# A hybrid decoder block on one core: the recurrence's coefficient on ScalarE, the input weights' low parts in two pieces on GpSimd

## The chip, the core and the metric

The kernel runs on one core of a Trainium2 chip. A core has five engines with queues of their own: TensorE (PE in the profile; its weight loads are PEld), VectorE (DVE), ScalarE (ACT), GpSimd (POOL) and SyncE (SP), which issues most of the DMAs. The metric is the device time of one execution in microseconds (us), as a median over runs.

## What is computed

The reference is one decoder block in float32 over 512 positions of 1024 channels. Cut to what matters here:

```
h = rmsnorm(x);  z = h @ w_in + b_in          # 1024 -> 6656 columns
z_glu, z_rx, z_rg, z_ga, z_gb = split(z)      # 2048, 1280, 1280, 1024, 1024
u  = glu(z_glu); u = causal depthwise conv, 31 taps; layernorm; silu
xb = causal depthwise conv of z_rx, 4 taps
r  = sigmoid(block_diag(wa) xb + ba);  i = sigmoid(block_diag(wx) xb + bx)
log_a = -8 * r * softplus(-lambda);  a = exp(log_a)
h_t = a_t * h_(t-1) + sqrt(1 - a_t^2) * (i * xb)_t          # the recurrence
y_a = u @ conv_w_out + b;  y_b = (h * gelu(z_rg)) @ lru_w_out
x  = x + (sigmoid(z_ga) * y_a + sigmoid(z_gb) * y_b) @ w_mix_out
x  = x + (silu(h2 @ w1) * (h2 @ w3)) @ w2;  out = rmsnorm(x)    # h2 = rmsnorm(x)
```

## The kernel before

Channels lie on the 128 partitions, the 512 positions along the free dimension. Every float32 operand of a product is split in two parts, a high one (a rounded copy in the format that TensorE multiplies) and a low one (the operand minus its high part). A product is then three matmuls: high by high, high by low, low by high.

The input product is done in 52 groups of 128 columns of z. A group is 8 slices of the contraction by 3 matmuls, 24 matmuls of 512 positions, into one PSUM bank (`mm3`, lines 534 to 546). There are six such banks in one pool, and two in another for the long convolution. The weights of a group come as one chunk of 128x1024 by a DMA that SP issues (line 175). `emit_chunk` asks ScalarE to copy the high part (line 124) and GpSimd to subtract for the low part (`split_to`, then `sub` on line 120). The weights are asked for four chunks ahead of their use (`AHEAD`), and there are four tiles of raw weights (`RAW`) and five of split ones (`HL`). The first two chunks, in the opening that is ordered by hand, are subtracted by GpSimd in halves already (`InHalves`, line 155). Chunks of later stages name VectorE for the low part.

The list `ORDER` interleaves the groups by kind: u (the gated input of the long convolution), rx (input of the short convolution and of the recurrence), g (the recurrence's gates), r (the recurrence itself), rg, gb and ga (the other branches). `beside` is a generator of the long convolution's steps: 31 taps by 8 tiles of channels on VectorE (line 743), of which a few are issued after each group. `make_out_sums` lets GpSimd add and subtract quarters of the last weight matrix in 256-column pieces (lines 447 and 120, tile `ows`), tied behind the newest subtraction of a chunk by `newest["sub"]`.

The function that the first half of the change touches is `gates(j)`, called ten times. Four to six matmuls per gate fill two banks, `r_` and `i_`, whose tile name in the profile is `g`. ScalarE takes tanh of both (lines 873, 874; a sigmoid as half of one plus tanh), then an exponential into the tile `A` (`ea` in the profile, line 877) and another tanh into the bank `r_` (line 878). VectorE forms (A + 1) * r_ in the bank (line 879), which is a - 1, and (i_ + 1) * xb (line 880). Line 881 writes the recurrence's coefficient a = r_ + 1 into `A`, and line 882 writes (A + 1) * r_ = a^2 - 1 into `th`. `recur(j)`, some groups later, takes the square root on ScalarE into a bank (line 890), multiplies by xb (line 891) and scans along the positions (line 892).

Only a few stretches are ordered by hand (`manual_schedule`: the opening and the ends of the mix product). Elsewhere the framework's scheduler writes each engine's queue beforehand, from the order of the program and from times that it estimates, and sets the semaphores for data, buffers and banks. On the chip each queue is executed in order. The rest of the block (the output products, the mix product in seven quarter products, the channel mixer likewise) follows in the same manner on the same engines.

Of the kernel before, what the change touches and what calls it, by code (L numbers as in the profile page):

```python
# [8 lines left out]
F32 = mybir.dt.float32  # L9
F32R = mybir.dt.float32r  # L10
AF = mybir.ActivationFunctionType
ALU = mybir.AluOpType

P = 128
T = 512
# [72 lines left out]
def tile_block(ctx, tc, a, out):  # L88
# [19 lines left out]
    def bank(name):  # L108
        return psum.tile([P, T], F32, tag="mm", name=name)
# [4 lines left out]
    vec, act, pe, pool_e = nc.vector, nc.scalar, nc.tensor, nc.gpsimd  # L114
# [4 lines left out]
    def sub(eng, o, x, y):  # L119
        return eng.tensor_tensor(out=o, in0=x, in1=y, op=ALU.subtract)  # L120

    def split_to(h, l, full, eng, copy=act.copy):

        copy(h, full)  # L124
        if eng is vec and "tie" in newest:
            with tc.issue_after(newest["tie"]):
                last = sub(eng, l, full, h.bitcast(F32))
        else:
            last = sub(eng, l, full, h.bitcast(F32))
        if eng is pool_e:  # L130
            newest["sub"] = last.ins
        return h, l, last

    def split(name, full, eng, p_=None, copy=act.copy):
        p_ = p_ or pairt(name)
        return split_to(*p_, full, eng, copy)[:2]
# [21 lines left out]
    def emit_chunk(copy=act.copy, lo_by=None):  # L158
        if emitted[0] == GATES_AT:
            load_gates()  # L160
        key, src, kt, cols, where, lo, after = chunks[emitted[0]]
        emitted[0] += 1
        lo = lo_by or lo
        n = kt * cols
        if where == "made":
            raw = src()
        else:
            raw = raws.tile([P, 1024], F32, tag="raw", name=f"raw_{key}")
        rv = raw[:, :n]
        if where == "made":  # L170
            pass
        elif callable(src):
            src(raw)
        else:
            newest["load"] = nc.sync.dma_start(rv.rearrange("p (k n) -> p k n", k=kt), src).ins
        if where != "long":
            hl = hls.tile([P, 2, 1024], F32R, tag="hl", name=f"hl_{key}")
            h, l, _ = split_to(hl[:, 0, :n], hl[:, 1, :n], rv, lo, copy)
            if after:
                after(rv, h)  # L180
            held[key] = (h.rearrange("p (k n) -> p k n", k=kt), l.rearrange("p (k n) -> p k n", k=kt))
        else:
            held[key] = [
                split_to(longt(f"{key}h{i}", F32R), longt(f"{key}l{i}", F32R), rv[:, i * T : (i + 1) * T], lo)
                for i in range(2)
            ]
# [5 lines left out]
    def weights(key, ahead=AHEAD):  # L192
        i = next(i for i, c in enumerate(chunks) if c[0] == key)
        emit_to(i + 1 + ahead)
        return held.pop(key)
# [657 lines left out]
    def gates(j):  # L853
        hv, lv = (gate_view(v[:, 0, :]) for v in weights(f"gate{j}"))
        j5 = j % 5
        banks = []
        for g in range(2):
            ps = bank(f"g{j}_{g}")
            (wh, oh), (wl, ol) = ((v[:, g, 0, :], v[:, g, 1, :]) for v in (hv, lv))
            xh, xl = xbp[j]  # L860
            mms = [(wh, xh), (wh, xl), (wl, xh)]
            if j5 % 2:
                eh, el = ext[j]
                mms += [(l[:MANY], r[:MANY]) for l, r in ((oh, eh), (oh, el), (ol, eh))]
            else:
                mms.append((oh[: 3 * FEW], ext[j][0][: 3 * FEW]))
            for k, (l, r) in enumerate(mms):
                pe.matmul(ps, l, r, start=k == 0, stop=k == len(mms) - 1)  # L868
            banks.append(ps)

        r_, i_ = banks
        th = gatet(f"th{j}")
        act.activation(th, r_, AF.Tanh, scale=0.5, bias=bh[:, 0, j : j + 1])
        act.activation(i_, i_, AF.Tanh, scale=0.5, bias=bh[:, 1, j : j + 1])

        A = gatet(f"ea{j}")
        act.activation(A, th, AF.Exp, scale=c8[:, j : j + 1], bias=c8[:, j : j + 1])
        act.activation(r_, th, AF.Tanh, scale=c4[:, j : j + 1], bias=c4[:, j : j + 1])
        vec.scalar_tensor_tensor(out=r_, in0=A, scalar=1.0, in1=r_, op0=ALU.add, op1=ALU.mult)
        vec.scalar_tensor_tensor(out=xb[j], in0=i_, scalar=1.0, in1=xb[j], op0=ALU.add, op1=ALU.mult)  # L880
        vec.tensor_scalar(out=A, in0=r_, scalar1=1.0, scalar2=None, op0=ALU.add)
        vec.scalar_tensor_tensor(out=th, in0=A, scalar=1.0, in1=r_, op0=ALU.add, op1=ALU.mult)
        rec[j] = A, th

# [25 lines left out]
    for kind, j in ORDER:  # L910
        next(sums_steps, None)
        if kind == "u":
            glu(j)
        elif kind == "rx":
            rx(j)
            run_beside(4)
        elif kind == "g":
            gates(j)
        elif kind == "r":
            recur(j)  # L920
        elif kind == "rg":
            rg(j)
            run_beside(6)
        elif kind == "gb":
            sig(GB, j, sgb, "sgb")
            run_beside(6)
        else:
            sig(GA, j, sga, "sga")
            run_beside(8)
# [237 lines left out]
    with tc.manual_schedule(engines={ET.PE}):  # L1167
        ws = w_tiles(f"f1_{PLAIN}", ND, 0)
        for q in range(4):
            cs, ks = HALVES[q // 2], range(4 * (q % 2), 4 * (q % 2) + 4)  # L1170
# [211 lines left out]
```

## Time and profile before

| | us |
|---|---|
| median of three runs | 795.95 |
| lowest and highest run | 795.84, 796.22 |
| span of the profiled execution | 794.7 |
| TensorE busy in it | 786.6 |
| VectorE busy | 688.9 |
| ScalarE busy | 473.8 |
| GpSimd busy | 221.9 |

The profiled execution is one run; its own time in the trace is the span from its first to its last instruction, 794.7 us, and 1.25 us lie between that and the median. A row of instructions reads: line of the kernel, engine, operation, tile written <- tiles read, shape, count; then total busy time and mean nanoseconds of one; then the engine's idle time before them and what ended it. A row of the timeline starts with the start and the length in microseconds. TensorE's matmuls overlap, so that one lasts 0.39 us in the trace while the next one starts after 0.23 us.

### The profile page before, as it was taken

Reading aid. Unit: us, or ns where it says so; the run is one execution under the profiler, and the core shown is the slowest. Engines: PE = TensorE matmul, PEld = TensorE weight load, DVE = VectorE, ACT = ScalarE, POOL = GpSimd, SP = SyncE. Lnnn points to the kernel's source line nnn. Section 1 sums busy time; section 2 is a strip of 40 time slices with the busy share of each in tenths; the row PEclk is TensorE's granted clock in tenths of the full one; section 3 lists DMA queues with packets and bytes.
Section 4 is the critical chain, followed back from the end, with each engine's and each line's share of the span. In section 5 each row is a group of like instructions: output and inputs, shape, how many; then the busy total and the mean of one; then the engine's idle time right before and its main releaser. Section 6 shows DMA issues by size and latency. Waiting matters only on the chain.

```text
span 794.7 us, 12042 instructions
## 1 busy us (share of the span) xinstructions
PE 786.6 (99%) x4300; PEld 686.4 (86%) x4300; DVE 688.9 (87%) x1047; ACT 473.8 (60%) x695; POOL 221.9 (28%) x174
## 2 busy tenths in 40 slices
PE   8999999999999999999999999999999999999997
PEld 8888888888888888888888898999999999888886
DVE  6699899999989988786887889979888888989867
ACT  7645685987768855563335575545455555585544
POOL 1865766797666856030000000000000000000000
PEclk9999999999999999999999999999999999999999
DMA  7955646487564664359847545655333332686552
GB/s 209 247 145 145 193 139 206 121 247 208 170 206 138 206 189 119 129 192 276 271 159 247 173 133 159 182 152 164 114 108 107 106 106 81 200 287 201 186 172 106
DMA packets 184603, 137.14 MB, mean 173 GB/s; under 512 B 14259, under 2 KB 163167, under 8 KB 184543
## 3 DMA queue, kind: packets, MB, share of 16 engines
q1 hardware_dynamic: 184255, 135.32, 56.3%
q0 software_dynamic: 288, 1.05, 0.7%
q8 instruction: 34, 0.56, 0.3%
q14 instruction: 26, 0.21, 0.1%
HBM read 113.79 MB, written 18.64 MB: 167 GB/s over the span
## 4 chain that ended last, share of the span: by engine, by line
PE 92%; DMA 3%; DVE 3%; ACT 1%; issue 0%; SPq 0%; ACTq 0%; POOLq 0%; DVEq 0%
PE z L544 35%; PE or L1003 12%; PE yb L544 7%; PE ft L1141 7%; PE fa L1141 7%; PE ya L544 5%; PE mxr L1003 5%; PE fr L1141 3%; PE g L868 3%; PE fb L1141 2%; PE fe L1151 2%; PE f L544 1%; DMA raw_fb<-raw_fb 1%; PE fe L1152 1%; DMA raw_fb<-in_ffn_w_dram 1%; PE f L1175 1%
## 5 line engine op out<-in xcount | busy, mean ns | idle before, releaser
L743 DVE SCALAR_TENSOR_TENSOR cv<-u,par,cv 128x511 f32<-128x511 f32 (+19 forms) x240 | 162.4, 731 | 6.0 <-ACT cv L740 5.7
L120 POOL TENSOR_TENSOR hl_in<-raw_in,hl_in 128x1024 fp32r<-128x1024 f32 x50 | 121.1, 2427 | 73.7 <-ACT hl_in L124 67.8
L120 POOL TENSOR_TENSOR ows<-ows 128x256 f32<-128x256 f32 x66 | 56.5, 858 | 37.9 <-DMA ows<-in_ffn_w_dram 34.9
L124 ACT CAST hl_ft<-raw_fb 128x1024 fp32r<-128x1024 f32 x40 | 41.9, 1050 | 31.7 <-DVE raw_fb L365 14.8
L124 ACT CAST hl_in<-raw_in 128x1024 fp32r<-128x1024 f32 x50 | 52.0, 1043 | 12.7 <-PE z L544 6.6
L120 DVE TENSOR_TENSOR hl_ft<-raw_fb,hl_ft 128x1024 fp32r<-128x1024 f32 x40 | 48.6, 1220 | 9.4 <-ACT hl_ft L124 9.4
L363 POOL DMA_DIRECT2D raw_fb<-raw_fb x2 | 1.9, 928 | 158.1 <-DVE raw_fb L365 158.1
L120 DVE TENSOR_TENSOR hl_fb<-raw_fb,hl_fb 128x1024 fp32r<-128x1024 f32 x30 | 36.7, 1223 | 8.4 <-ACT hl_fb L124 8.0
L544 PE MATMUL z<-h10h,hl_in 128*128 128x512 f32 (+1 forms) x106 | 41.1, 388 | 0.2 <-DVE h10l L600 0.2
L544 PE MATMUL z<-h12h,hl_in 128*128 128x512 f32 (+1 forms) x106 | 40.6, 384 | 0.0
L544 PE MATMUL z<-h14h,hl_in 128*128 128x512 f32 (+1 forms) x106 | 40.6, 384 | 0.0
L544 PE MATMUL z<-h17h,hl_in 128*128 128x512 f32 (+1 forms) x106 | 40.6, 384 | 0.0
L544 PE MATMUL z<-h11h,hl_in 128*128 128x512 f32 (+1 forms) x106 | 40.6, 383 | 0.0
L544 PE MATMUL z<-h16h,hl_in 128*128 128x512 f32 (+1 forms) x106 | 40.6, 383 | 0.0
L544 PE MATMUL z<-h13h,hl_in 128*128 128x512 f32 (+1 forms) x106 | 40.6, 383 | 0.0
L544 PE MATMUL z<-h15h,hl_in 128*128 128x512 f32 (+1 forms) x106 | 40.6, 383 | 0.0
L365 DVE TENSOR_TENSOR raw_fb<-raw_fb,raw_fb 128x1024 f32<-128x1024 f32 x28 | 34.2, 1222 | 7.0 <-DMA raw_fb<-in_ffn_w_dram 6.7
L124 ACT CAST hl_fb<-raw_fb 128x1024 fp32r<-128x1024 f32 x30 | 31.4, 1047 | 8.6 <-PE mxr L1003 3.7
L124 ACT CAST hl_ob<-raw_ob 128x1024 fp32r<-128x1024 f32 (+1 forms) x23 | 23.3, 1015 | 19.6 <-PE or L1003 10.5
L120 DVE TENSOR_TENSOR hl_ob<-raw_ob,hl_ob 128x1024 fp32r<-128x1024 f32 (+1 forms) x23 | 27.1, 1176 | 6.3 <-ACT hl_ob L124 4.4
L1141 PE MATMUL ft<-hs_1h,hl_ft 128*128 128x256 f32 x160 | 30.4, 284 | 0.0
L124 ACT CAST hl_ot<-raw_ot 128x1024 fp32r<-128x1024 f32 (+1 forms) x17 | 17.5, 1027 | 17.8 <-PE or L1003 16.8
(1082 smaller groups left out, 2630.7 us busy)
## 6 DMA issues: line engine op xcount, KB each, us to landing
raw_in<-in_w_in_dram SPq DMA_DIRECT2D x52, 512.0 KB
raw_fb<-in_ffn_w_dram SPq DMA_DIRECT2D x96, 256.0 KB
ows<-in_ffn_w_dram SPq DMA_DIRECT2D x44, 256.0 KB
os<-ows SPq DMA_DIRECT2D x22, 512.0 KB
raw_ob<-in_ffn_w_dram SPq DMA_DIRECT2D x33, 256.0 KB
raw_ot<-os SPq DMA_DIRECT2D x33, 256.0 KB
raw_lo<-in_lru_w_out_dram SPq DMA_DIRECT2D x16, 320.0 KB
x<-in_x_dram SPq DMA_DIRECT2D x16, 256.0 KB
```

What stands on the lines that cost most here:

```text
L120: return eng.tensor_tensor(out=o, in0=x, in1=y, op=ALU.subtract)
L124: copy(h, full)
L363: pool_e.dma_start(out=q, in_=y, accum_op=ALU.add)
L365: vec.tensor_tensor(out=q, in0=q, in1=y, op=ALU.add)
L544: pe.matmul(ps, l, r, start=i == 0, stop=i == n - 1)
L743: vec.scalar_tensor_tensor(out=acc[c][:, s:], in0=u[c][:, : T - s], scalar=dw(c, s), in1=acc[c][:, s:], op0=ALU.mult, op1=ALU.add)
L868: pe.matmul(ps, l, r, start=k == 0, stop=k == len(mms) - 1)
L1003: pe.matmul(banks[i], l_[:, ts], r_, start=start and n == 0, stop=stop and n == 2, skip_group_check=again)
L1141: pe.matmul(ps[:, HALVES[i]], lw[:, 4 * i + c, :], rx_, start=not (again or i or c or m), stop=bool(i and c == 3 and m == 2), skip_group_c ...
L1151: pe.matmul(ps, h[:, 4 * i + c, :], both_[c], start=c == 0, stop=False, skip_group_check=True)
L1152: pe.matmul(ps[:, LO], l[:, 4 * i + c, :], xh, start=False, stop=c == 3, skip_group_check=True)
L1175: pe.matmul(plain_1[:, cs], l, r, start=k == 0 and m == 0, stop=k == ND - 1 and m == 2)
```

## The change

The coefficient `A` = r_ + 1 of each gate is written by an Identity activation with bias 1.0 on ScalarE, no longer by an add on VectorE. And where GpSimd subtracts for the low part of a chunk with 1024 columns, it does so by two instructions of 512 columns each. That holds for the 50 chunks of the input weights behind the first two; the gates' chunks have 512 columns and stay whole. What is tied behind a chunk's subtraction is tied behind the second piece.

```diff
@@ -125,6 +125,9 @@
         if eng is vec and "tie" in newest:
             with tc.issue_after(newest["tie"]):
                 last = sub(eng, l, full, h.bitcast(F32))
+        elif eng is pool_e and full.shape[-1] == 2 * T:
+            for cs in (slice(0, T), slice(T, 2 * T)):
+                last = sub(eng, l[:, cs], full[:, cs], h[:, cs].bitcast(F32))
         else:
             last = sub(eng, l, full, h.bitcast(F32))
         if eng is pool_e:
@@ -878,7 +881,7 @@
         act.activation(r_, th, AF.Tanh, scale=c4[:, j : j + 1], bias=c4[:, j : j + 1])
         vec.scalar_tensor_tensor(out=r_, in0=A, scalar=1.0, in1=r_, op0=ALU.add, op1=ALU.mult)
         vec.scalar_tensor_tensor(out=xb[j], in0=i_, scalar=1.0, in1=xb[j], op0=ALU.add, op1=ALU.mult)
-        vec.tensor_scalar(out=A, in0=r_, scalar1=1.0, scalar2=None, op0=ALU.add)
+        act.activation(A, r_, AF.Identity, bias=1.0)
         vec.scalar_tensor_tensor(out=th, in0=A, scalar=1.0, in1=r_, op0=ALU.add, op1=ALU.mult)
         rec[j] = A, th
```

## The prediction

> **What bounds the kernel now.** I read the page's first part, then TensorE's (PE's) waits, then busy time by stretches, then the chain of waits.
>
> ```profile
> span 794.7 us, 12042 instructions
> ...
> PE 786.6 (99%) x4300; PEld 686.4 (86%) x4300; DVE 688.9 (87%) x1047; ACT 473.8 (60%) x695; POOL 221.9 (28%) x174
> ```
>
> PE is busy for all but 794.7 - 786.6 = 8.1 us. The other engines, the three that the change touches, have time over on the average. Where do the 8.1 us lie?
>
> ```profile
> PE warm L514 <- DVE ones L507: 1.1, 1, 1.1
> PE par_ps L525 <- DMA rows<-in_norm_g_dram: 0.9, 1, 0.9
> PE tx L576 <- DVE x L619: 0.4, 1, 0.4
> PE z L544 <- DVE h10l L600: 0.2, 1, 0.2
> PE fr L1141 <- ACT ft L1262: 0.2, 1, 0.2
> ```
>
> ```profile
> 0.00:10.00 10.00, 7.61 (x43) 7.19 (x44) 2.98 (x11) 6.27 (x16) 0.70 (x6) 1.00 0.83 236
> ...
> 24.00:320.00 296.00, 296.00 (x1310) 245.11 (x1310) 276.34 (x421) 203.26 (x257) 207.98 (x160) 1.00 0.60 176
> ...
> 782.00:795.00 13.00, 7.38 (x42) 6.27 (x40) 8.00 (x24) 6.07 (x20) 0.00 (x0) 0.98 0.44 163
> ```
>
> The first list is complete: five waits, 2.8 us, and four of them come before the stage of the input products, which is where the change acts (24 to 320 us). In the stretches (window, length, then busy time of PE, PEld, DVE, ACT and POOL; behind them the granted clock, 1.00 in the stage), 10.00 - 7.61 = 2.4 us are lost before the first product and 13.00 - 7.38 = 5.6 us behind the last one, while the output's last rows are normed and stored. From 24 to 320 us nothing is lost: 296.00 of 296.00; VectorE (DVE) is the next fullest with 276.34. So inside the stage that is changed there is no wait of PE that a better DVE, ScalarE (ACT) or GpSimd (POOL) could remove; the change can only lose there, or leave it.
>
> A busy PE in this profile is a modelled one, so the matmuls' pace has to be looked at too. Two pieces of the chain give it:
>
> ```profile
> 243.37 65.30 PE z L544 x288
> ...
> 327.26 47.60 PE yb L544 x210
> ```
>
> 65.30 / 288 = 0.2267 us and 47.60 / 210 = 0.2267 us. The first piece lies in the changed stage, beside a crowded DVE and a working POOL; the second lies behind it, with other weights. The pace is the same to the fourth digit, so it is PE's own and not set by what runs beside it.
>
> **The change part by part.** The rows of the operations taken away, and those nearest to the ones added:
>
> ```profile
> L881 DVE TENSOR_SCALAR ea<-g 128x512 f32<-128x512 f32 x10 | 6.8, 684 | 0.1
> ...
> L819 ACT ACTIVATE xb<-z,par 128x512 f32<-128x512 f32 x10 | 7.8, 780 | 0.0
> L816 ACT ACTIVATE z<-z,par 128x512 f32<-128x512 f32 x10 | 6.6, 658 | 10.4 <-PE z L544 10.4
> L899 ACT ACTIVATE sgb<-z,par 128x512 f32<-128x512 f32 x8 | 5.5, 688 | 0.1
> ...
> L120 POOL TENSOR_TENSOR hl_in<-raw_in,hl_in 128x1024 fp32r<-128x1024 f32 x50 | 121.1, 2427 | 73.7 <-ACT hl_in L124 67.8 <-issue 2.9 <-DMA raw_in<-in_w_in_dram 1.2
> L155 POOL TENSOR_TENSOR hl_in<-raw_in,hl_in 128x512 fp32r<-128x512 f32 x2 | 2.5, 1282 | 8.7 <-DVE hl_in L124 8.7
> ```
>
> *The coefficient.* Ten instructions leave DVE: 10 x 0.684 = 6.8 us less of its 276.34 us. Ten Identity activations come to ACT. The bounds for one are 0.658 us (L816, the same function, but PSUM to PSUM) and 0.780 us (L819, with a scale per partition, PSUM to SBUF). I take 0.69 us, the row of L899: it reads PSUM, writes SBUF and has no scale by pointer, as here. That is 6.9 us (6.6 to 7.8) more on ACT's 203.26 us in a stretch of 296. None of it is PE's. Identity in L816 has no table load on its line, so I add none. [...]
>
> *The waits that come with it.* L881 had only its own engine's result (L879) before it. Now ACT must wait for L879, and L882 on DVE must wait for ACT. Gate 4, where DVE is full, shows what stands around them:
>
> ```profile
> 146.43 1.04 ACT L124 CAST hl_in<-raw_in 128x1024 fp32r<-128x1024 f32 x1
> 147.37 0.77 ACT L819 ACTIVATE xb<-z,par 128x512 f32<-128x512 f32 x1
> 148.16 1.28 ACT L890 ACT_TABLE_LOAD   x1
> ...
> 146.07 0.69 DVE L879 SCALAR_TENSOR_TENSOR g<-ea,g 128x512 f32<-128x512 f32 x1
> 147.30 0.69 DVE L881 TENSOR_SCALAR ea<-g 128x512 f32<-128x512 f32 x1
> 148.33 0.69 DVE L882 SCALAR_TENSOR_TENSOR th<-ea,g 128x512 f32<-128x512 f32 x1
> ...
> 155.82 1.21 DVE L892 TENSOR_TENSOR_SCAN xb<-ea,mu 128x512 f32<-128x512 f32 x1
> ...
> 150.51 0.39 PE L544 MATMUL z<-h10h,hl_in 128*128 128x512 f32 x1
> ...
> 157.80 0.40 PE L544 MATMUL z<-h10h,hl_in 128*128 128x512 f32 x1
> ```
>
> L879 ends at 146.76 and L882 starts at 148.33, 1.57 us later. If ACT takes the coefficient behind the cast that is then under way (to 147.47), it is done at about 148.16, before L882 started. Queued behind it on ACT are the eviction L819, the table load and the square roots of the recurrence, each 0.69 us later; on DVE behind L882 stand the taps of the two convolutions.
>
> Who waits for that? PE does, through the six PSUM banks. Counting a bank as taken at the first matmul of its group (or the square root of the recurrence) and given back by its last reader, the closest margins of the stage are two. The group that starts at 150.51 has five banks taken around it and needs the sixth, which L882 of gate 4 gave back at 148.33 + 0.69 = 149.02: 1.5 us to spare. The group at 157.80 needs the one that the scan gave back at 155.82 + 1.21 = 157.03: 0.8 us. So the cover of the new waits is 0.8 to 1.5 us at its thinnest, and DVE gains 0.68 us per gate against it. I cost the waits at nothing; the upper bound is with the rivals.
>
> *The subtraction in two pieces.* 50 instructions become 100. By L155, which is such a piece, one takes 1.282 us: 2 x 1.282 - 2.427 = 0.14 us more per chunk, 50 x 0.14 = 6.9 us more on POOL's 207.98. Who waits for the low part? Every group of PE. The first chunk (the first of the two that start at 21.89) and the tightest one behind the start, each with the start of its group:
>
> ```profile
> 21.89 4.86 POOL L120 TENSOR_TENSOR hl_in<-raw_in,hl_in 128x1024 fp32r<-128x1024 f32 x2 [9.35 <-ACT hl_in L124]
> ...
> 154.12 2.81 POOL L120 TENSOR_TENSOR hl_in<-raw_in,hl_in 128x1024 fp32r<-128x1024 f32 x1
> ...
> 25.04 0.48 PE L544 MATMUL z<-h10h,hl_in 128*128 128x512 f32 x1
> ...
> 163.26 0.39 PE L544 MATMUL z<-h10h,hl_in 128*128 128x512 f32 x1
> ```
>
> The first ends at about 21.89 + 4.86 / 2 = 24.3, and its group starts at 25.04: 0.7 us to spare, of which the pieces take 0.14 for the second half alone, which is used half a group later. Afterwards it is 6.3 us at the least (156.93 to 163.26), and 0.14 us is nothing against that. If a matmul in the middle of a group now waits for the second piece, it carries a wait already fulfilled. The pace of the 12 groups above, each of which starts with such waits, is that of the groups behind them to under 0.01 us, so 50 more cost PE between 0 and about 0.1 us. I take 0.1.
>
> The pieces also change how DVE meets POOL:
>
> ```profile
> 107.56 2.41 POOL L120 TENSOR_TENSOR hl_in<-raw_in,hl_in 128x1024 fp32r<-128x1024 f32 x1 [4.30 <-ACT hl_in L124]
> ...
> 65.86 0.69 DVE L120 TENSOR_TENSOR xb2l<-xb,xb2h 128x512 fp32r<-128x512 f32 x1
> ...
> 108.25 2.26 DVE L120 TENSOR_TENSOR xb4l<-xb,xb4h 128x512 fp32r<-128x512 f32 x1
> ```
>
> The same subtraction of two SBUF operands on DVE takes 0.69 us alone and 2.26 us when it begins under one of POOL's, and it ends just after POOL's does (110.51 against 109.97). With pieces half as long the wait should be at most a piece: about 1.28 + 0.69 = 1.97 us, if DVE is let in between the pieces. That is a microsecond or two of DVE in the whole stage. It helps the margins, and PE has no wait that it could shorten.
>
> *The sum.* On PE's path: -0 (no wait removed) + 0.1 (waits fulfilled) + 0 (new waits covered). The profiled execution's span 794.7 becomes 794.8 us. The median of the runs, 795.95, is 1.25 us above that span; I leave this difference as it is. 794.8 + 1.25 = 796.05, given as 796.0. About 0.2% of this, 1.6 us, is what a measurement of this kernel can tell from no change.
>
> **The rivals.**
>
> *Slower: ACT stands still at the coefficient.* ACT's queue is in order, and its order is planned beforehand by estimated times. If the coefficient stands right behind L878 in it, ACT waits until DVE gets to L879. At gate 3 that is long:
>
> ```profile
> 124.40 0.77 ACT L878 ACTIVATE g<-th,c 128x512 f32<-128x512 f32 x1
> ...
> 132.92 0.69 DVE L879 SCALAR_TENSOR_TENSOR g<-ea,g 128x512 f32<-128x512 f32 x1
> ...
> 138.58 0.74 DVE L821 SCALAR_TENSOR_TENSOR xb<-z,par,xb 128x509 f32<-128x509 f32 x1
> ...
> 145.07 0.39 PE L544 MATMUL z<-h10h,hl_in 128*128 128x512 f32 x1
> ...
> 139.41 0.62 ACT L124 CAST xb5h<-xb 128x512 fp32r<-128x512 f32 x1 [6.22 <-DVE xb L821]
> ```
>
> From 125.17 to 133.61 is 8.4 us in which the next evictions on ACT would wait, those of rx5 first. Its bank is what decides: L821 gives it back at 138.58 + 0.74 = 139.32, and by the same count of banks PE takes it again at 145.07, 5.8 us later. PE would lose 8.4 - 5.8 = 2.6 us: 798.6. ACT's own idle 6.22 us before the cast of xb5 then takes up most of what is left. It decides from a stand of 5.8 + 1.6 = 7.4 us on. For it: DVE lags ACT by that much in this place. Against it: the plan puts ACT's dependent work late, behind idle time like these 6.22 us, so it seems to know how far DVE lags. The milder form, the coefficient behind the cast, eviction and table load of gate 4 (1.04 + 0.77 + 1.28, to 149.44), gives L882's end at about 150.9, 1.9 us later than now; against margins of 1.5 and 0.8 us that costs up to 1.1 us, 797.1, still no measurable change. Chance of a loss over 1.6 us by the strong form: 0.09.
>
> *Slower: another order further on.* Queues outside the parts ordered by hand are planned as a whole, so moved work can reorder what follows, where PE is as full as here. One operand late by a microsecond or three gives 797 to 799. Nothing in the profile asks for it. Chance of more than 1.6 us: 0.05.
>
> *Faster: PE has room that its busy time hides.* Weight loads are busy for 245.11 of the 296.00 us, 83%. If matmuls were held up by 17% and a freer DVE let go of a twentieth of that, 296 x 0.17 x 0.05 = 2.5 us would go: 793.5. [...] The equal pace of 0.2267 us in and behind the stage speaks against such room, and no wait is left to go in the stage. Chance 0.03.
>
> *No effect at all*, because the planner keeps the old order and the pieces run back to back: the same 796.0; it is within the forecast's case.
>
> **How the numbers follow.** Forecast (the change is hidden, up to the milder stall): 0.83; slower by over 0.2%: 0.09 + 0.05 = 0.14; faster by over 0.2%: 0.03. The range runs from 795.2 (0.8 us below, should a small wait of PE at the ends shift) to 797.8 (the milder stall at 797.1 and the near end of the second rival); the strong stall and the gain are left out.
>
> **What would show it.** In the changed profile: ten Identity activations on ACT near 690 ns and no more table loads; ten fewer DVE instructions; 100 POOL subtractions near 1.28 us; PE still 296.00 of 296.00 in 24 to 320 us and no new line in its list of waits; xb's low parts on DVE never over about 2 us. It is wrong if PE's list shows a wait for ACT, DVE or POOL of more than a microsecond in the stage, or if the two pieces of the chain lose their pace of 0.2267 us.

## The result, and the profile after

The changed kernel takes 804.12 us (four runs, 803.67 to 804.86) against 796.0 us of the kernel before (795.84 to 796.22): ratio 1.0101, 95% interval 1.0089 to 1.0113. It is slower by 8.1 us; the forecast was no measurable change, and its range ended at 797.8.

The new code makes lines behind the first hunk three higher: 881 is now 884, 740 is 743, 819 is 822, 843 is 846, 868 is 871. The experiments below change single lines and keep the old numbers. First the page of the changed kernel, its head and the group of the pieces (count, busy us, mean ns):

```profile
span 803.0 us, 12095 instructions
...
PE 790.3 (98%) x4300; PEld 687.4 (86%) x4300; DVE 681.0 (85%) x1037; ACT 480.2 (60%) x706; POOL 228.4 (28%) x224
...
L120 POOL TENSOR_TENSOR hl_in<-raw_in,hl_in 128x512 fp32r<-128x512 f32 x100 | 130.0, 1324 | 75.1 <-ACT hl_in L124 63.8 <-DMA ext<-xb3h 4.1 <-issue 3.1
```

The engines' counts are as forecast but for one table load: ten instructions fewer on DVE, ACT 11 more (the ten coefficients and that load), 50 more on POOL. The loss does not show there. It shows in PE's waits of the changed kernel (all of 0.3 us and more):

```profile
PE g L871 <- DMA ext6h<-xb7h: 1.7, 1, 1.7
PE g L871 <- ACT ext L846: 1.3, 1, 1.3
PE warm L517 <- DVE ones L510: 1.1, 1, 1.1
PE z L547 <- DVE xb L883: 1.0, 1, 1.0
PE fe L1144 <- DVE hl_ft L120: 0.8, 1, 0.8
PE g L871 <- DMA ext6l<-xb7l: 0.6, 1, 0.6
PE tx L579 <- DVE x L622: 0.3, 1, 0.3
```

Four of these lie in the stage of the input products, which had none. The stage's length is a better measure than the list: from the first matmul of 512 positions with `h10h` to the first one of `yb`. Before it ran from 25.04 to 319.85 us, 294.81 us; now, by PE's timeline,

```profile
24.60 0.48 PE L547 MATMUL z<-h10h,hl_in 128*128 128x512 f32 x1
...
157.67 0.47 PE L871 MATMUL g<-ext,hl_gate 96*128 96x512 f32 x1 [1.31 <-ACT ext L846]
...
181.18 0.39 PE L871 MATMUL g<-xb6h,hl_gate 128*128 128x512 f32 x1
183.32 0.49 PE L871 MATMUL g<-ext6h,hl_gate 112*128 112x512 f32 x1 [1.75 <-DMA ext6h<-xb7h]
184.46 0.77 PE L871 MATMUL g<-ext6l,hl_gate 112*128 112x512 f32 x1 [0.65 <-DMA ext6l<-xb7l]
185.02 0.63 PE L871 MATMUL g<-ext6h,hl_gate 112*128 112x512 f32 x1
185.45 0.63 PE L871 MATMUL g<-xb6h,hl_gate 128*128 128x512 f32 x1
...
187.95 0.39 PE L547 MATMUL z<-h10h,hl_in 128*128 128x512 f32 x1
...
260.87 0.50 PE L547 MATMUL z<-h10h,hl_in 128*128 128x512 f32 x1 [0.98 <-DVE xb L883]
...
327.00 0.39 PE L547 MATMUL yb<-y0h,hl_lo 128*128 128x512 f32 x1
```

327.00 - 24.60 = 302.40 us, 7.59 more. The start is 0.44 earlier (in the kernels below it varies from 23.8 to 25.0), so 7.15 us show up at 327.00; of the 8.3 us by which the span grew, the other 1.2 come later, 0.8 of them in the wait for `hl_ft` at the start of the feed-forward part. What the reader sees in the rows:

- At gate 5 the third `ext` copy of ACT is late: 1.31 us.
- At gate 6 two operands are late, 1.75 and 0.65 us. From 181.18 to 187.95 are 6.77 us for ten steps; at the pace of 0.23 us they take 2.31. So 4.46 us go here, more than the 2.40 us of the two waits, because the matmuls behind the waits start every 0.43 us instead of 0.23. The windows of the changed kernel (length, PE busy, granted clock, DMA share, GB/s) show why:

```profile
180.00:184.00 4.00, 2.06 (x8) 1.00 0.85 259
...
184.50:187.90 3.40, 3.40 (x8) 0.50 0.85 248
```

TensorE was granted half its clock for 3.40 us after the waits, which makes 1.70 us of work late without a wait that any list shows. PE counts as busy meanwhile (3.40 of the 3.40 us), which is a good part of why its busy time went *up*, from 786.6 to 790.3 us.

- At 260.87 a bank comes back 0.98 us late from gate 9.

**Why the operands of gate 6 are late.** `ext6` holds rows of `xb7`, the short convolution's output of the seventh rx group, so the path is ACT's first tap of rx7 (the eviction `xb<-z,par`), DVE's three taps, ACT's cast `xb7h`, DVE's `xb7l`, and two DMAs that SP issues. ACT's timeline of the kernel before, then of the changed one:

```profile
166.35 0.78 ACT L819 ACTIVATE xb<-z,par 128x512 f32<-128x512 f32 x1
...
167.97 1.50 ACT L740 ACTIVATE cv<-u,par 128x512 f32<-128x512 f32 x2
169.51 0.62 ACT L124 CAST xb7h<-xb 128x512 fp32r<-128x512 f32 x1
```

```profile
159.60 0.78 ACT L743 ACTIVATE cv<-u,par 128x512 f32<-128x512 f32 x1
...
170.64 0.60 ACT L884 ACTIVATE ea<-g 128x512 f32<-128x512 f32 x1 [1.76 <-DVE g L882]
171.13 0.78 ACT L822 ACTIVATE xb<-z,par 128x512 f32<-128x512 f32 x1
...
175.97 0.62 ACT L124 CAST xb7h<-xb 128x512 fp32r<-128x512 f32 x1 [1.48 <-DVE xb L824]
```

`cv<-u` is the first tap of the long convolution's third pair of channel tiles. Before, both of the pair begin behind rx7's eviction. Now one of them begins 8.4 us earlier, ahead of it. The moved coefficient stands 1.76 us in ACT's queue for DVE, with rx7's eviction behind it. What keeps DVE is in its own timeline, before and after:

```profile
164.44 0.68 DVE L879 SCALAR_TENSOR_TENSOR g<-ea,g 128x512 f32<-128x512 f32 x1
...
167.17 2.32 DVE L821 SCALAR_TENSOR_TENSOR xb<-z,par,xb 128x511 f32<-128x511 f32 x3 [0.59 <-ACT xb L819]
...
170.71 1.06 DVE L120 TENSOR_TENSOR xb7l<-xb,xb7h 128x512 fp32r<-128x512 f32 x1
```

```profile
160.42 5.47 DVE L746 SCALAR_TENSOR_TENSOR cv<-u,par,cv 128x511 f32<-128x511 f32 x7 [0.57 <-ACT cv L743]
...
169.91 0.69 DVE L882 SCALAR_TENSOR_TENSOR g<-ea,g 128x512 f32<-128x512 f32 x1
...
172.53 0.74 DVE L824 SCALAR_TENSOR_TENSOR xb<-z,par,xb 128x511 f32<-128x511 f32 x1
...
177.10 0.68 DVE L120 TENSOR_TENSOR xb7l<-xb,xb7h 128x512 fp32r<-128x512 f32 x1
```

Eleven taps of the third pair, ready early (the seven of this row and four more), stand ahead of gate 5's step, where eight of the second pair stood before; the step runs 5.5 us later. rx7's taps and `xb7l` follow, 5.4 and 6.4 us later, the taps now with others between them. By SP's timelines the DMAs `ext6h` and `ext6l` are issued at 174.22 and 174.87 us before, at 179.93 and 181.58 after. In the changed kernel `ext6h` was there 183.32 - 179.93 = 3.4 us after its issue; by this it had been there at 177.6 before, against its use at 180.26: 2.7 us of margin, used up by 5.7 us of delay (gate 6 itself began 1.15 us later, behind gate 5's wait). The order of PE's queue is the same in both kernels; only the others' changed.

The issue of `ext6h` does not follow directly on `xb7h`, which was done at 175.97 + 0.62 = 176.59. SP's queue and the end of POOL's sums, in the changed kernel:

```profile
179.23 0.60 SPq L455 DMA_DIRECT2D os<-ows  x1
179.93 0.58 SPq L851 DMA_DIRECT2D ext6h<-xb7h  x1
```

```profile
178.46 0.74 POOL L120 TENSOR_TENSOR ows<-ows 128x256 f32<-128x256 f32 x1
```

Ahead of the transfer stands the store of `ows`, and SP waits 3.3 us for it, until POOL's last sum ends at 178.46 + 0.74 = 179.20. POOL's sums stand behind the subtraction of a chunk that starts at 172.92, when ACT has ended the cast of this chunk (171.80 + 1.05 = 172.85); and ACT does that cast behind the coefficient and rx7's eviction. So the late ACT queue reaches gate 6 by two ways, through `xb7h` and through POOL and SP, and the second is the later one. Before, the same store stood there too: `xb7h` was done at 170.13, the sums at 173.18, and `ext6h` was issued at 174.22. An estimate: issued as soon as `xb7h` was done, and with the same 3.4 us, `ext6h` would have been there at about 180.0, ahead of its use at 183.32 - 1.75 = 181.57. No kernel here moves the store alone, so its share of the loss is not shown.

### The profile page after: what moved, and what is told of

Its sections match the earlier page's. It is cut to its first block, busy times and chain, and to the rows that moved or that the text cites. A ratio compares the mean times of both kernels' runs of the same rounds, so it can differ in the third digit from the quotient of the medians.

```text
span 803.0 us, 12095 instructions
## 1 busy us (share of the span) xinstructions
PE 790.3 (98%) x4300; PEld 687.4 (86%) x4300; DVE 681.0 (85%) x1037; ACT 480.2 (60%) x706; POOL 228.4 (28%) x224
## 3 DMA queue, kind: packets, MB, share of 16 engines
q0 software_dynamic: 288, 1.05, 0.7%
## 4 chain that ended last, share of the span: by engine, by line
PE 73%; DVE 18%; DMA 3%; ACT 2%; issue 2%; POOL 2%; SPq 0%; ACTq 0%; POOLq 0%; DVEq 0%
PE z L547 19%; PE or L1006 12%; DVE cv L746 10%; PE yb L547 7%; PE ft L1144 6%; PE fa L1144 6%; PE ya L547 5%; PE mxr L1006 5%; PE fr L1144 3%; PE fb L1144 2%; PE fe L1154 2%; PE f L547 1%; POOL hl_in L120 1%; PE fe L1155 1%; DVE xb L824 1%
## 5 line engine op out<-in xcount | busy, mean ns | idle before, releaser
L746 DVE SCALAR_TENSOR_TENSOR cv<-u,par,cv 128x499 f32<-128x499 f32 (+19 forms) x240 | 166.1, 731 | 7.7 <-ACT cv L743 6.2
L120 POOL TENSOR_TENSOR hl_in<-raw_in,hl_in 128x512 fp32r<-128x512 f32 x100 | 130.0, 1324 | 75.1 <-ACT hl_in L124 63.8
L120 POOL TENSOR_TENSOR ows<-ows 128x256 f32<-128x256 f32 x66 | 54.1, 823 | 41.1 <-DMA ows<-in_ffn_w_dram 38.1
```

Of the source, the lines that this page charges most:

```text
L746: vec.scalar_tensor_tensor(out=acc[c][:, s:], in0=u[c][:, : T - s], scalar=dw(c, s), in1=acc[c][:, s:], op0=ALU.mult, op1=ALU.add)
```

## The experiments

The theory (A, where the expectations use letters): the coefficient on ScalarE makes the planner write another order of ACT's and DVE's queues, the third pair ahead of gate 5 and rx7, and that order is the cost. The rivals: the handover itself at gates 4 and 5 (B: ACT standing at the coefficient, DVE waiting for ACT), the pieces, or the DVE time set free. The table has each kernel's ratio to the kernel before on the same chip, the stage's length beyond 294.81 us, and PE's waits in the stage of 0.3 us and more (gate 9 is the wait for the bank of gate 9 that line 880 gives back, near 255 to 260 us; sg the wait for ACT's line 805 near 230 us).

| kernel | median, us | ratio (95%) | stage, us | waits in the stage, us |
|---|---|---|---|---|
| the change | 804.12 | 1.0101 (1.0089 to 1.0113) | +7.59 | gate 5 1.3; gate 6 2.4; gate 9 1.0 |
| coefficient alone | 802.86 | 1.0082 (1.0067 to 1.0097) | +7.01 | y0l 0.3; gate 6 2.7; gate 9 1.1 |
| pieces alone | 796.6 | 1.0005 (0.9995 to 1.0014) | 0.00 | none |
| both, not gates 4 and 5 | 804.47 | 1.0097 (1.0080 to 1.0113) | +9.62 | gate 6 4.9; gate 9 1.1 |
| pieces, gates 0 to 3 | 803.38 | 1.0100 (1.0083 to 1.0117) | +7.33 | gate 6 4.5; gate 9 0.3 |
| pieces, gates 6 to 9 | 796.98 | 1.0006 (0.9995 to 1.0017) | +0.33 | none |
| pieces, gates 5 to 9 | 798.88 | 1.0033 (1.0021 to 1.0044) | +2.05 | sg 0.5; gate 9 0.7 |
| pieces, gate 5 | 796.17 | 0.9999 (0.9990 to 1.0008) | 0.00 | none |
| both, the old add kept idle | 806.29 | 1.0124 (1.0109 to 1.0139) | +10.04 | gate 5 0.7; gate 6 3.3; gate 9 1.1; others 1.5 |
| before, taps earlier | 805.59 | 1.0122 (1.0107 to 1.0137) | +8.79 | gate 6 5.5 |
| both, third pair tied | 799.87 | 1.0050 (1.0035 to 1.0065) | +3.60 | gate 5 1.3; sg 0.5; gate 9 0.7 |
| coefficient alone, tied | 799.11 | 1.0037 (1.0023 to 1.0050) | +2.72 | y0l 0.3; sg 0.5; gate 9 0.7 |
| both, tied, not gate 5 | 800.34 | 1.0052 (1.0039 to 1.0065) | +3.58 | gate 5 1.3; sg 0.5; gate 9 0.7 |

**The coefficient alone.**

```diff
-        vec.tensor_scalar(out=A, in0=r_, scalar1=1.0, scalar2=None, op0=ALU.add)
+        act.activation(A, r_, AF.Identity, bias=1.0)
```

> The coefficient on ScalarE alone, the subtraction whole. Theory A (the queues were planned anew: the taps of the long convolution got ahead of the gates' work, so that the extra operands of gates 5 and 6 come late): 802 to 806 us, with PE waiting for the copies of gate 5 or the transfers of gate 6. Theory B (ScalarE stands at the coefficient and holds the eviction behind it): the same 802 to 806. Theory C (the pieces make VectorE's two-operand subtraction wait, 1.46 us for xb6's low part, and that starts it): 796 to 799.

802.86 us, with the third pair's first tap at 159.94 and PE's wait at gate 6. It carries the loss by itself, and nearly all of it: 7.01 of 7.59 us of the stage.

**The pieces alone.**

```diff
-            last = sub(eng, l, full, h.bitcast(F32))
+            last = [sub(eng, l[:, c], full[:, c], h[:, c].bitcast(F32)) for c in (slice(0, T), slice(T, 2 * T))][-1] if eng is pool_e and full.shape[-1] == 2 * T else sub(eng, l, full, h.bitcast(F32))
```

> The subtraction in two pieces alone, the coefficient on VectorE. Theories A and B: 795.5 to 797 us and no wait of PE in the stage. Theory C: 798 to 804 with PE waiting for gate 5's copies.

796.6 us over ten runs, 1.0005: no change. The stage has its old length to the hundredth, and the third pair begins at 167.59, behind rx7's eviction (165.97). By themselves the pieces are what the prediction said of them.

**Both, with the coefficient of gates 4 and 5 on VectorE.** This takes the handovers away that stand next to the late operands.

```diff
+        act.activation(A, r_, AF.Identity, bias=1.0) if j not in (4, 5) else vec.tensor_scalar(out=A, in0=r_, scalar1=1.0, scalar2=None, op0=ALU.add)
```

> As changed, but gates 4 and 5 write their coefficient on VectorE. In ScalarE's queue nothing waits for VectorE ahead of the eviction of rx7 any more, while the order in which the next pair of the long convolution starts is still the changed one. Theory B: the waits of gate 6 (2.3 us and the slow matmuls behind them, 1.6 us) go, 798 to 800 us. Theory A: they stay, 802 to 805 us.

804.47 us; no recovery. The wait at gate 5 is gone, that at gate 6 has doubled, and half the clock is granted for twice as long. PE's waits, ACT's timeline and the windows of PE:

```profile
PE g L868 <- DMA ext6h<-xb7h: 4.9, 1, 4.9
```

```profile
159.58 0.78 ACT L740 ACTIVATE cv<-u,par 128x512 f32<-128x512 f32 x1
...
169.72 0.78 ACT L819 ACTIVATE xb<-z,par 128x512 f32<-128x512 f32 x1
...
174.38 0.62 ACT L124 CAST xb7h<-xb 128x512 fp32r<-128x512 f32 x1 [2.23 <-DVE xb L821]
```

```profile
183.60:190.50 6.90, 6.42 (x15) 0.51 0.77 172
```

No coefficient stands in front of rx7's eviction here, and it is late all the same, while the early third pair is there again. So the handover at the place of the loss isn't its cause. The way through SP shows here too: `xb7h` is done at 175.00, and its transfer is issued at 179.36, behind a load of input weights that waits for POOL until 178.90.

**Which gates.** Pieces, and the coefficient on ScalarE at gates 0 to 3, 6 to 9, 5 to 9, or 5 alone; the condition is all that differs.

```diff
+        act.activation(A, r_, AF.Identity, bias=1.0) if j < 4 else vec.tensor_scalar(out=A, in0=r_, scalar1=1.0, scalar2=None, op0=ALU.add)
```

> The pieces, and the coefficient on ScalarE for gates 0 to 3 only; in the planned order the third pair starts ahead of gate 5. Theory A: PE waits over 1.5 us at gate 6, 799.5 to 805 us. A cost in proportion to the gates moved: 0.4 of 8.1 us, 799.3 us, with no single place.

> The pieces, and the coefficient on ScalarE for gates 6 to 9 only; in the planned order the third pair stays behind rx7. Theory A: no wait at gate 6, 796 to 798.5 us. A cost in proportion: 799.3 us.

> The pieces, and the coefficient on ScalarE for gates 5 to 9. Gate 5's stands right ahead of rx7's eviction on ScalarE, as in the changed kernel, but the third pair starts behind rx7 in the planned order, as before. Theory A: no wait of PE at gate 6, 795.5 to 798.5 us. If ScalarE standing at gate 5's coefficient costs by itself: a wait at gate 6 and 799 to 803 us.

> The pieces, and the coefficient on ScalarE at gate 5 alone; the other nine stay on VectorE. What is open is where the 2 us come from that are left when gates 5 to 9 are moved and that gates 6 to 9 alone do not show: a wait of PE for ScalarE's sg near 230 us (0.5), one for VectorE's xb near 255 us (0.7) and one for hl_ft at the start of the feed-forward part (0.6). Theory, the order that follows gate 5: the planner answers gate 5's handover with another order of what comes behind it, so gate 5 alone gives the same waits and 798.0 to 799.5 us. Rival, each gate pays for its own handover: no wait near 255 us, where gate 9's coefficient is on VectorE again, and 796.0 to 797.3 us.

Gates 0 to 3 alone cost as much as the whole change (803.38 us), though from gate 4 on this kernel has the old code: the third pair begins at 160.25, and PE waits 4.5 us at gate 6. The kernels without gates 0 to 3 have the pair behind rx7 and no wait at gate 6. Gates 6 to 9, and gate 5, cost nothing that can be told from no change. Gates 5 to 9 cost 2.05 us of the stage; the wait at gate 6 is gone as expected, but 798.88 us is 0.4 above the expected range. Gate 5 alone does not show those 2 us, so the theory of an order that follows from gate 5's handover fell: 796.17 us, the rival's figure. In PE's waits of the kernel with gates 5 to 9

```profile
PE z L544 <- DVE xb L880: 0.7, 1, 0.7
PE fe L1141 <- DVE hl_ft L120: 0.6, 1, 0.6
PE z L544 <- ACT sg L805: 0.5, 1, 0.5
```

the two of the stage belong to neither gate 5 alone nor gates 6 to 9 alone; here it took both.

**Both, with the old add kept as an idle step.** DVE gets its ten adds back; they write 1 + r_ into `th`, which the next line overwrites.

```diff
+        act.activation(A, r_, AF.Identity, bias=1.0); vec.tensor_scalar(out=th, in0=r_, scalar1=1.0, scalar2=None, op0=ALU.add)
```

> As changed, and VectorE also does the old add, into the tile that its next operation overwrites, so that its work is what it was. If the freed time of VectorE is what moved the taps forward (the narrow form of theory A): back to 795.5 to 797.5 us. If the wait between the engines is what moved them, or theory B: 802 to 806 us.

806.29 us, no faster than the change (and 0.3 us above the range expected for this case); the third pair begins at 164.16, ahead of rx7's eviction (174.79). So the loss doesn't need the 6.8 us that DVE is given back. That narrow form of the theory, taps that slip into freed time, fell; a planner that reacts to the wait between the engines remains possible, but no run isolates it.

**Before, with 14 taps emitted earlier.** No coefficient and no subtraction is changed; the program only lists taps of the long convolution sooner (8 more behind rx6, 6 behind rg1) and fewer later, in one function's three calls, of which one is

```diff
-            run_beside(4)
+            run_beside(4 + {'rg1': 6, 'u5': 0, 'rx6': 8, 'gb3': -6, 'rg2': -6, 'rx8': -2}.get(f"rx{j}", 0))
```

> The kernel before, coefficient on VectorE and subtraction whole, but 14 taps of the long convolution are issued some groups earlier (8 more after rx6, 6 more after rg1, and 6, 6 and 2 fewer after gb3, rg2 and rx8), so that the third pair starts ahead of gate 5 in the planned order. Theory A: PE waits at gate 6 here too, 798 to 805 us, without any of the change. If the coefficient on ScalarE is needed for the loss: 795.5 to 797.5 us.

805.59 us. ACT's timeline and PE's wait:

```profile
163.18 1.49 ACT L740 ACTIVATE cv<-u,par 128x512 f32<-128x512 f32 x2
...
171.55 0.77 ACT L819 ACTIVATE xb<-z,par 128x512 f32<-128x512 f32 x1
...
176.16 0.62 ACT L124 CAST xb7h<-xb 128x512 fp32r<-128x512 f32 x1 [2.90 <-DVE xb L821]
```

```profile
PE g L868 <- DMA ext6h<-xb7h: 5.3, 1, 5.3
```

An order with the third pair ahead of rx7 makes the loss alone, with both halves of the change absent (805.59 us is 0.6 above the expected range). This is the run that shows the cause of gate 6's part. Its order was made by hand and is not the changed kernel's in every step: both taps of the pair come early here. And here too `ext6h` is issued well after `xb7h` is done (180.90 against 176.78), behind a load that waits for POOL.

**The third pair tied behind rx7.** Three kernels in which ACT's first tap of the third pair is issued behind rx7's eviction: the changed kernel, the one with the coefficient alone, and the changed one with gate 5's coefficient on VectorE.

```diff
-                act.activation(acc[c], u[c], AF.Identity, scale=dw(c, 0), bias=pc("conv_dw_b", c))
+                with tc.issue_after(newest["rx7"]) if c0 == 4 else ExitStack(): act.activation(acc[c], u[c], AF.Identity, scale=dw(c, 0), bias=pc("conv_dw_b", c))
...
-        act.activation(o, ps, AF.Identity, scale=lw(0), bias=pc("lru_conv_b", j))
+        newest[f"rx{j}"] = act.activation(o, ps, AF.Identity, scale=lw(0), bias=pc("lru_conv_b", j)).ins
```

> As changed, but the start of the long convolution's third pair is tied behind the eviction of rx7 in ScalarE's queue, where it stood before the change. Theory A (the third pair's taps got ahead of gate 5 and rx7 on VectorE, so that the operands of gate 6 come late): PE's wait at gate 6 goes with the slow matmuls behind it, 796.5 to 800.5 us. If the cost is the work and the waits that the coefficient brings to ScalarE: 802 to 806 us, the wait at gate 6 stays.

> The tied kernel, but with the subtraction whole. If PE's 1.3 us at gate 5 in the tied and the changed kernel come from VectorE's subtraction of xb6 meeting GpSimd's pieces: that wait goes, 797 to 799.5 us. If it comes from the coefficient alone: it stays, 799 to 801 us.

> The changed kernel with the third pair of the long convolution tied behind the eviction of rx7 in ScalarE's queue, and with gate 5's coefficient back on VectorE. Theory, the order that follows gate 5: the waits near 230 and 255 us and the one for gate 5's own ext go, 796.0 to 797.5 us. Rival, each gate pays for its own handover: the wait for xb near 255 us stays (gate 9's coefficient is on ScalarE), 798.0 to 800.0 us, as the tied kernel without this (799.9).

The tie alone takes the changed kernel's stage from +7.59 to +3.60 us. In ACT's timeline and PE's windows of the tied kernel `xb7h` is in time again and the clock is whole:

```profile
168.83 0.77 ACT L819 ACTIVATE xb<-z,par 128x512 f32<-128x512 f32 x1
...
170.43 1.49 ACT L740 ACTIVATE cv<-u,par 128x512 f32<-128x512 f32 x2
172.04 0.62 ACT L124 CAST xb7h<-xb 128x512 fp32r<-128x512 f32 x1
```

```profile
184.00:186.00 2.00, 2.00 (x11) 1.00 0.84 256
```

The tie changes SP's queue as well: `ext6h` is issued at 173.96 here, ahead of the store of `ows` (176.67). In the tied kernel with gate 5 on VectorE the store comes first again (176.28), and `ext6h`, issued at 176.98, is still in time. What is left is gate 5's wait and the waits for sg and gate 9. With the coefficient alone, tied, gate 5's wait is gone. Gate 5's row in the table has a plain pattern: it is there in the four kernels that have both the pieces and gate 4's coefficient on ScalarE, and in none of the others. Handing gate 5's coefficient back does not help (800.34 us, where 796.0 to 797.5 had been expected by the theory and 798.0 to 800.0 by the rival): the wait at gate 5 takes gate 4's handover, not gate 5's. How it meets the pieces is seen on DVE and POOL, in the changed kernel:

```profile
154.70 1.54 DVE L120 TENSOR_TENSOR xb6l<-xb,xb6h 128x512 fp32r<-128x512 f32 x1
```

```profile
154.41 2.96 POOL L120 TENSOR_TENSOR hl_in<-raw_in,hl_in 128x512 fp32r<-128x512 f32 x2 [1.76 <-ACT hl_in L124]
```

`xb6l` begins under a piece and takes 1.54 us; in the tied kernel with whole chunks it begins at 154.93 and takes 0.68, ahead of POOL's subtraction at 155.28. POOL starts in both when ACT has cast the chunk, and that is 0.5 us later into the stage in the second. So in these two kernels the rows differ, 1.54 and 0.68 us, with which of the two comes first; that the pieces as such hold `xb6l` is not shown. Two of ACT's `ext` copies wait for it and for each other. Before, the last copy ahead of gate 5's first `ext` matmul ended at 155.95, 0.68 us ahead of its use at 156.63; in the changed kernel it ends at 157.52. Part of this is not the pieces': the coefficient-alone kernels lose 0.65 us ahead of gate 5 instead, at `y0l` among others (from the stage's start to gate 5's first matmul 131.5 us against 130.9 before and after).

## Why the prediction was wrong

The step that failed is "I cost the waits at nothing", with its ground, the margins of 0.8 and 1.5 us "at its thinnest": the term "new waits covered", put at 0, became a stage that is 7.59 us longer. Two things were wrong in it.

- *The list of margins.* It followed the banks and, for the pieces, the weight chunks. A gate's matmuls also need `xb`'s parts and the `ext` copies, and those had 0.7 us at gate 5 and some 2.7 us (high part) at gate 6. Gate 5's was thinner than the thinnest that was counted, and it was reached. Among the banks, too, one was missed. In the kernel before, gate 9's bank is given back at 252.71 + 0.69 = 253.40 and taken again at 254.11, 0.7 us later; that group is the one that waits at 260.87 in the changed kernel:

```profile
252.71 0.69 DVE L880 SCALAR_TENSOR_TENSOR xb<-g,xb 128x512 f32<-128x512 f32 x1
...
254.11 0.39 PE L544 MATMUL z<-h10h,hl_in 128*128 128x512 f32 x1
```

- *The order of the queues as given.* The bound added up durations along the old order, "each 0.69 us later", and ended at 797.1. In the new order gate 6's transfer from rx7 was issued 5.7 us later, eight times the 0.69 us that the prediction gave the coefficient.

The loss by its parts, in the stage: gate 6 4.46 us (2.40 of waits, 1.70 at half clock, the rest around the waits), gate 5 about 1.5, gate 9's bank and what follows it about 1.5 (0.98 of wait, the rest slower steps around it and before the next group): 7.5 of 7.59. Gate 6's part is shown to be the order, from both sides: put there without the change (+8.79) and taken out of it by one tie (-3.99). Which link of the new order carries it, `xb7h` or what stands ahead of its transfer in SP's queue, stays open; by the rows the latter came last. Gate 5's part takes the pieces and gate 4's coefficient together, and why gate 9's bank is late is not shown.

Other steps, in their order:

- *PE has no wait to lose in the stage; the change can only lose there, or leave it.* Right; but a stage with 296.00 of 296.00 us busy also has no room for a late operand, and that should have weighed more in the chances.
- *The coefficient, 0.69 us on ACT.* It took 0.594 us (ten, 583 to 599 ns), under the lower bound of 0.658. Cheaper than on DVE (0.684 us), and of no help.
- *No more table loads.* One more, 47 against 46, because the order splits a pair of square roots: before, both start at 149.46 us or just behind, after one load; now they start at 148.34 and 152.23, each after a load of 1.28 us.
- *The pieces, +6.9 us on POOL, nothing on PE.* The group takes 130.0 us against 121.1, +8.9 us (1324 ns a piece, not 1282); alone they cost PE nothing. Together with gate 4's handover there is a wait. One reading was off without harm: behind the first chunk the margin was not "6.3 us at the least", since the second chunk, which ends at 21.89 + 4.86 = 26.75, is used from 30.59 on, 3.8 us later.
- *DVE's subtraction beside POOL at most 1.97 us.* Right: the longest is 1.54, down from 2.34; the ten together 9.62 against 11.69 us.
- *The rival "ACT stands still at the coefficient", 0.09.* It stands at four gates, 8.8 us in all, at gate 3 for 4.9, without a wait of PE at the bank of rx5 that it named. At gate 5 its 1.76 us do lie on the path to `xb7h`, but with the coefficients of gates 4 and 5 on DVE `ext6h` was issued as late (155.5 us into the stage against 155.3).
- *The rival "another order further on", 0.05.* This is what happened. "Nothing in the profile asks for it" was the error: the profile shows the old order, and not how the planner, which works from estimated times, answers a new step. It was priced as one operand late by 1 to 3 us; the reordering hit operands of two gates and a bank, and at gate 6 alone it cost 4.46 us, since the loss at half clock, 1.70 us, comes on top of the waits of 2.40.
- *Faster, from hidden room.* Nothing of it: outside the waits and the slow clock the step stayed at 0.227 us. That the 17% of the stage without weight loads could be room was the author's estimate; no run shows it.

Left open: which property of the new step makes the planner start the third pair earlier (the kernel with the idle add shows only that it isn't the freed time), why the waits for sg and gate 9 come with earlier gates moved and not with gates 6 to 9 alone, and the wait for `hl_ft`, which came in five kernels (0.6 to 0.8 us in four of them) and not by any one part of the change. No kernel here beats the one before; the pieces equal it, alone or with the coefficient of gate 5 or of gates 6 to 9.

## What to carry to other kernels

Where a scheduler writes the queues, moving one instruction to another engine can change the whole order, and a sum along the old order is no bound. Before moving it, list for the fully busy engine every operand's margin, not only banks and weights; and compare the built queues afterwards, for filler work that has become ready earlier and stands ahead of what the full engine needs next. Look at the queue that issues the DMAs as well: a transfer whose data are ready can stand behind a store that waits for another engine, as `ext6h` did here for 3.3 us. A single tie of the filler behind that work took half of this loss back.

## What the runs showed of the hardware

In the stage of the input products the granted clock stayed at 1.00 behind PE's short waits and fell with the long ones. In the changed kernel it was 1.00 from 157.67 to 161.00 us, behind the wait of 1.31 us at gate 5, and 1.00 from 260.87 to 264.00, behind the 0.98 us for gate 9's bank. Behind the 2.40 us at gate 6 (1.75 and 0.65, one matmul apart) it was 0.50 from 184.50 to 187.90, and 1.00 again from 188.00 to 190.00. In the tied kernel with gate 5 on VectorE, whose waits in the stage were 1.3, 0.7 and 0.5 us, its mean over the whole span was 1.0. The wait of 4.5 us (gates 0 to 3) was followed by 0.50 from 185.00 to 188.40. With the waits of 4.9 us (gates 4 and 5 on VectorE) and 5.3 us (taps earlier) it was 0.51 from 183.60 to 190.50, and it had begun to fall before the wait ended: 0.95 from 180.00 to 184.00, a window in which no matmul ran.

No run varies the length of a wait alone, so it is not shown what length between 1.31 and 2.40 us is enough, nor what sets the time at half clock. The slow clock cost 1.70 us above the waits in the changed kernel (half of 3.40). With gates 4 and 5 on VectorE it cost an estimated 3.1 us, from 6.42 us of busy PE at 0.51.
